# Residual rows of the last but one down group loaded from GpSimd's queue, and the last pair's product placed behind two of that group's additions

## The chip, the cores and the metric

The kernel runs on one core of one Trainium2 chip. The metric is the device time of one execution in microseconds. Engines are named as in the profile: PE is TensorE (matrix products), DVE is VectorE, ACT is ScalarE, POOL is GpSimd, SP is SyncE, which here only issues transfers.

## The reference

One decoder layer over 1040 positions (16 learned ones ahead of 1024) of width 1024: an RMS norm, a mixer (a gated convolution branch and sparse attention, merged and added to the stream), then the convolutional feed-forward part around which this change lies, and a last RMS norm.

```
h = rms_norm(stream, ffn_norm_g[l])
up = causal_depthwise_conv(h @ ffn_up[l], ffn_dw_w[l], ffn_dw_b[l])     # 2 x 2816 columns, width 3
a, b_ = jnp.split(up, 2, axis=-1)
stream = stream + (jax.nn.silu(a) * b_) @ ffn_down[l]
out = rms_norm(stream, final_norm_g)
return out[:, N_META:]
```

## The kernel before

Everything lies channel by partition: a tile is 128 channels by positions. A float32 matrix is split into a high and a low part in TensorE's rounded format, and each product is made in three passes (high x high, high x low, low x high).

**The up part.** The 2816 columns of each half are 22 tiles; tile i of the one half and tile i of the other are a pair. A pair needs seven half-size products (`A11`, `A12`, `A22`, `N2`, `S3`, `S1`, `S4`; the scheme of seven products in place of eight), each of 24 matmuls against the tiles in `B` (`B11`, `B21`, `T4`, `T2`, `T3`, `T1`, `B22`, in this order). `up_pair` adds them up on VectorE into `ua` and `ub`; the last of these additions takes `S4`. `up_rows` makes the rows that the down part reads: three taps of the convolution for each half (the first on ScalarE, L1139, two on VectorE, L1141) into `us` and `ut`, the Silu on `us` (ScalarE, L1142), the product of the halves (VectorE, L1143), a cast of it to the high part `uh` (ScalarE, L1145) and the rest, `ul` (VectorE, L1146).

**The down part.** Two pairs make a group (`GT` = 2), so there are 11 groups. For each group, `down` makes eight products (m = 0 to 7, one for each 128 output channels), each of 12 matmuls of 512 columns, three passes by two pairs by two halves of the positions. Groups 0 to 8 are copied out of PSUM and added in HBM to the residual stream `d_x2` by an accumulating transfer from POOL's queue (L1171). Before group 9, the last but one, `d_x2` is loaded into eight tiles `x2` (named x_0 to x_7 in the profile; L1193), and the products of group 9 (of pairs 18 and 19) are added to them on VectorE (L1167). Group 10, of pairs 20 and 21, comes last and is not made by `down`: it goes in three chunks of positions (384, 384, 256 columns), each followed by its norm and its output, so that a matmul of 384 columns marks its beginning.

**What sets the order.** The instructions of each engine stand in one queue. Which order they get is decided when the program is built, by a planner that follows the data, the priority (the order of the code; `urgent()` raises it by 600 places) and its own estimate of times. Weights pass through `raw` tiles (`d` for the down weights, loaded on SP's queue, L1033) and are split into a ring of five blocks, high part on ScalarE (L1065), low part on VectorE (L1066). PSUM has eight banks, and `slot()` hands out four slots of two banks each in turn, to up and down products alike: the product m + 4 can only begin when the addition of m has read its slot. The tiles `x2` come from a pool of 31 (`ft`) and take the places of the tiles in `B` that are no longer read.

Of the kernel before, what the change touches and what calls it, by code (L numbers as in the profile page):

```python
# [16 lines left out]
ALU = mybir.AluOpType  # L17
# [6 lines left out]
SEQ = 1024  # L24
# [16 lines left out]
GT = 2  # L41
# [39 lines left out]
def body(ctx: ExitStack, tc: tile.TileContext, xT, vecs, w_idx, w_v, w_conv, w_k, w_q, w_gate,  # L81
         w_pw, w_o, w_merge, w_up, w_down, tab128, tab64, topk_rows, mask0, mask_tiny, out):
    nc = tc.nc
    dve, act, pool, pe = nc.vector, nc.scalar, nc.gpsimd, nc.tensor

    def f(t):
        return t.bitcast(F32)

    def urgent():
        return tc.high_priority(offset=600)  # L90
# [8 lines left out]
    def ft(name, dtype=F32):  # L99
        return base.tile([P, FW], dtype, tag="F", bufs=NF, name=name)  # L100

    def tmp(name, dtype=F32):
        return base.tile([P, FW], dtype, tag="T", bufs=4, name=name)
# [10 lines left out]
    def wload(i):  # L114
        src, nk = wlist[i]
        raw = base.tile([P, KT * P], F32, tag="wr", bufs=2, name=f"wr{i}")
        nc.sync.dma_start(raw[:, :nk * P], src)
        wh = base.tile([P, KT * P], F32R, tag="wh", bufs=3, name=f"wh{i}")
        wl = base.tile([P, KT * P], F32R, tag="wl", bufs=2, name=f"wl{i}")
        with urgent():  # L120
            act.copy(wh[:, :nk * P], raw[:, :nk * P])  # L121
            if i < 2 or i >= ix_mg[0][0]:
                placed[0] = dve.tensor_tensor(wl[:, :nk * P], raw[:, :nk * P], f(wh)[:, :nk * P], op=ALU.subtract)
            else:
                act.activation(wl[:, :nk * P], raw[:, :nk * P], AF.Copy, scale=-1.0)
                pool.dma_start(wl[:, :nk * P], src, accum_op=ALU.add)
        wdone[i] = (wh, wl)
# [36 lines left out]
    NPAIR = DFF // P  # L164
# [11 lines left out]
    def c3(ap, w):  # L176
        return ap.rearrange("p (c n) -> p c n", n=w)
# [16 lines left out]
    def psm():  # L194
        turn["mm"] ^= 1
        return PS[:, 3 * turn["mm"]:3 * turn["mm"] + 3, :]

    def bank(key, banks):
        i = turn.get(key, 0)
        turn[key] = i + 1  # L200
        return PS[:, banks[i % len(banks)], :]
# [22 lines left out]
    def vcol(i):  # L224
        return vec[:, i:i + 1]
# [33 lines left out]
    for c in range(NCH):  # L259
# [19 lines left out]
        for k in range(KT):  # L279
            x = xs[k][:, cs]  # L280
# [50 lines left out]
    def rope(ps, ct, st, half, name, c0=0, w=CW, nch=NCH, adder=None):  # L331

        n = w * nch
        sw = tmp(name + "s")
        t = tmp(name + "t")
        with urgent():
            for b in range(0, P, 2 * half):
                act.copy(c3(sw[b:b + half, :n], w), ps[b + half:b + 2 * half, :nch, :w])
                act.copy(c3(sw[b + half:b + 2 * half, :n], w), ps[b:b + half, :nch, :w])
            dve.tensor_tensor(c3(t[:, :n], w), ps[:, :nch, :w], c3(ct[:, c0:c0 + n], w), op=ALU.mult)  # L340
            pool.tensor_tensor(sw[:, :n], sw[:, :n], st[:, c0:c0 + n], op=ALU.mult)
            if adder is None:
                pool.dma_start(t[:, :n], sw[:, :n], accum_op=ALU.add)
            else:
                adder.tensor_tensor(t[:, :n], t[:, :n], sw[:, :n], op=ALU.add)
        return t
# [175 lines left out]
    def table128():  # L522
        if not rt:
            rt[:] = [rope_table("c128", tab128[0]), rope_table("s128", tab128[1])]
        return rt
# [93 lines left out]
    for kind, i, w in units:  # L619
        if kind == "conv":  # L620
            ps = PS[:, 0:3, :] if i == 1 else psm()
# [11 lines left out]
            if i == 0:  # L633
                ps = psa
            else:
                ps = PS[:, 0:3, :] if i == 1 else psm()
                mm(ps, wget(w[1]), hh, hl, KT, LCOLS)
            g = ft(f"g{i}")
# [20 lines left out]
        else:  # L659
            ps = PS[:, 0:3, :] if kind == "g" and i < FILL0 else psm()  # L660
# [6 lines left out]
            elif kind == "k":  # L667
                mm(ps, wget(w), hh, hl, KT, LCOLS)
                t = rope(ps, *table128(), 64, f"kr{i}")
                act.copy(km[:, i * M0:(i + 1) * M0], t[:, :M0])  # L670
                nc.sync.dma_start(d_k[i], t[:, :LC])
            else:
                mm(ps, wget(w), hh, hl, KT, LQCOLS)
                t = rope(ps, *table128(), 64, f"qr{i}", c0=Q0, w=QW)
# [84 lines left out]
    for m in range(KT):  # L759
        tha = load_gate(m)  # L760
        ps = psm()
# [112 lines left out]
    for n in range(len(steps) + 2):  # L874
        if n < len(steps):
            h, p = steps[n]
# [12 lines left out]
    for h in range(NH):  # L889
        a, b = ft(f"oh{h}", F32R), ft(f"ol{h}", F32R)  # L890
# [7 lines left out]
    def ft2(name, dtype=F32):  # L898
        return f2.tile([P, 2 * HB], dtype, tag="F2", bufs=7, name=name)

    def slot():

        turn["sl"] = i = (turn.get("sl", -1) + 1) % 4
        return PS[:, 2 * i:2 * i + 2, :]
# [9 lines left out]
    for m in range(KT):  # L914
        thb, za = load_gate(KT + m), tmp(f"zar{m}")
        nc.sync.dma_start(za[:, :LQ], d_za[m])
        ps = psm()
# [3 lines left out]
        a, b = (ft2 if m == 7 else ft)(f"zh{m}", F32R), (ft2 if m == 7 else ft)(f"zl{m}", F32R)  # L921
# [6 lines left out]
    d_x2 = [dram.tile([P, SEQ], F32, name=f"dx2_{m}") for m in range(KT)]  # L928
# [143 lines left out]
    def block(i, n):  # L1072

        j = count["used"]
        assert bseq[j] == (i, n)
        while count["made"] < min(j + RB, len(bseq)):
            make_block()
        count["used"] += 1
        return ring[j % RB]
# [28 lines left out]
    def up_pair(i):  # L1108

        ua = tmp(f"ua{i}")  # L1110
        if i in early:
            act.copy(ua[:, :2 * HB], early.pop(i)[:, :2 * HB])
        else:
            up_first(i, ua)
        ub = tmp(f"ub{i}")
        U, U2 = ua[:, h1], ub[:, h1]

        def add(dst, a, ps, op=ALU.add):
            with urgent():
                dve.tensor_tensor(dst, a, ps, op=op)  # L1120

        p4 = prod(i, "A22", "T4")
        add(U, U, prod(i, "N2", "T2"), op=ALU.subtract)
        add(U2, U, prod(i, "S3", "T3"))
        add(ub[:, h0], U2, p4)
        p5 = prod(i, "S1", "T1")
        add(U2, U2, p5)
        add(U, U, p5)
        add(U, U, prod(i, "S4", "B22"))
        return ua, ub  # L1130

    def up_rows(i):

        ua, ub = up_pair(i)
        s_, t = ft2(f"us{i}")[:, :SEQ], ft2(f"ut{i}")[:, :SEQ]
        for j, u, d in ((2 * i, ua, s_), (2 * i + 1, ub, t)):
            wc = V_FW + 3 * j
            u, d = u[:, :2 * HB].rearrange("p (c n) -> p c n", n=HB), c3(d, HS)
            act.activation(d, u[:, :, 0:HS], AF.Identity, scale=vcol(wc), bias=vcol(V_FB + j))  # L1139
            for w in (1, 2):  # L1140
                dve.scalar_tensor_tensor(d, u[:, :, w:w + HS], vcol(wc + w), d, op0=ALU.mult, op1=ALU.add)  # L1141
        act.activation(s_, s_, AF.Silu)  # L1142
        dve.tensor_tensor(s_, s_, t, op=ALU.mult)  # L1143
        hi, lo = ft2(f"uh{i}", F32R), ft(f"ul{i}", F32R)
        act.copy(hi[:, :SEQ], s_)  # L1145
        dve.tensor_tensor(lo[:, :SEQ], s_, f(hi)[:, :SEQ], op=ALU.subtract)  # L1146
        return hi, lo

    def down_mm(ps, t, e, rows, c0, w):

        for pi, (o, x) in enumerate(((0, 0), (0, 1), (WB, 0))):
            for k in range(GT):
                for c in range(ps.shape[1]):
                    wo = o + (e * GT + k) * P
                    pe.matmul(ps[:, c, :w], lhsT=t[:, wo:wo + P], rhs=rows[k][x][:, c0 + c * w:c0 + (c + 1) * w],  # L1155
                              start=(pi == 0 and k == 0), stop=(pi == 2 and k == GT - 1))

    def down(g, rows, x2=None):

        for m in range(KT):  # L1160
            ps = slot()
            if m % 2 == 0:
                w = block(g * GT, m // 2)
            down_mm(ps, w, m % 2, rows, 0, HS)
            if x2:
                x = c3(x2[m][:, :SEQ], HS)
                dve.tensor_tensor(x, ps, x, op=ALU.add)  # L1167
            else:
                t = tmp(f"dn{g}_{m}")
                act.copy(c3(t[:, :SEQ], HS), ps)  # L1170
                pool.dma_start(d_x2[m], t[:, :SEQ], accum_op=ALU.add)  # L1171
# [9 lines left out]
    rows_second()  # L1181
    xs2.clear()
    rows = []
    for i in range(NPAIR):
        rows.append(up_rows(i))
        if i % GT == 0 and 0 < i < NPAIR - GT:
            down(i // GT - 1, rows[:GT])
            del rows[:GT]
    B.clear()

    x2 = [ft(f"x2_{m}") for m in range(KT)]
    for m in range(KT):
        nc.sync.dma_start(x2[m][:, :SEQ], d_x2[m])  # L1193
    down(NPAIR // GT - 2, rows[:GT], x2)
    del rows[:GT]


    wd = [block(NPAIR - GT, q) for q in range(4)]
    for c, (c0, nb) in enumerate(DCOLS):
# [4 lines left out]
        for m in range(KT):  # L1204
            ps = bank("dn", (0, 1, 2, 3))
# [105 lines left out]
```

## Time and the profile before

| | us |
|---|---|
| median of 3 runs | 1860.74 (1859.44 to 1862.48) |
| the profiled execution, its own time | 1865.77 |
| its span, from the first instruction to the last | 1863.7 |

The profile is of one execution. Its times are counted from the first instruction; what lies outside the span belongs to the start and the end of the launch. An instruction's length includes its way through the engine, so neighbours on one engine overlap a little: what an instruction costs in a row of equal ones is the distance of two starts. Only idle time of an engine that others wait for costs anything.

### The profile page before, as it was taken

What the parts mean: (1) busy time and instruction counts of PE and PEld (TensorE: products, weight loads), DVE (VectorE), ACT (ScalarE), POOL (GpSimd) and SP (SyncE); (2) the same over time, 40 slices, a digit from 0 to 9 for tenths busy, and PEclk for the clock granted to TensorE, in tenths of its full rate; (3) what the DMA queues carried; (4) which work ended last, traced back from release to release, by engine and by line L of the source; (5) the groups of instructions that cost most, each with busy time, mean ns of one, the idle gap of its engine ahead of it and who ended that gap; (6) DMA issues with size and microseconds to landing.
All of it is one profiled execution on the core that took longest, in us unless ns stands there. A gap on an engine that the chain in (4) does not pass through costs nothing. (4 is left out here: it accounts for less than half of the span.)

```text
span 1863.7 us, 29939 instructions
## 1 busy us (share of the span) xinstructions
PE 1790.6 (96%) x11956; PEld 1719.0 (92%) x11956; DVE 1231.9 (66%) x1949; ACT 1049.3 (56%) x1728; POOL 300.4 (16%) x310
## 2 busy tenths in 40 slices
PE   8989999999999999999999999899999999999987
PEld 7978899999999899899899999888999999999977
DVE  3598588997953472487843467845756575567677
ACT  3565587888999733488832246445434453444334
POOL 0243221111113122121100002011101100110002
PEclk7899999999999999999999999999999999999998
DMA  4434277776656488512246544365446634563432
GB/s 167 91 81 101 59 159 178 177 169 155 147 136 143 129 203 238 137 47 68 70 135 194 176 136 115 107 125 135 103 115 123 147 83 120 116 149 87 105 136 91
DMA packets 83899, 240.10 MB, mean 129 GB/s; under 512 B 8312, under 2 KB 28080, under 8 KB 83760
## 3 DMA queue, kind: packets, MB, share of 16 engines
q0 software_dynamic: 26208, 92.35, 27.9%
q1 hardware_dynamic: 57552, 145.84, 23.5%
q8 instruction: 93, 1.52, 0.3%
q14 instruction: 46, 0.38, 0.1%
HBM read 149.93 MB, written 65.09 MB: 115 GB/s over the span
## 5 line engine op out<-in xcount | busy, mean ns | idle before, releaser
L173 PE MATMUL PS<-hh,wh 128*128 128x342 f32 (+2 forms) x1096 | 196.0, 333 | 15.8 <-DVE qx0t L340 4.8
L1087 PE MATMUL PS<-B,ring 128*128 128x258 f32 (+1 forms) x1584 | 199.4, 286 | 5.5 <-DVE ub L1120 5.5
L1087 PEld LDWEIGHTS PS<-B,ring 128*128 128x128 f32 x1584 | 196.8, 193 | 8.2 <-DVE ub L1120 6.6
L173 PEld LDWEIGHTS PS<-hh,wh 128*128 128x128 f32 x1096 | 183.4, 195 | 20.2 <-DVE qx0t L340 5.2
L1155 PE MATMUL PS<-uh,ring 128*128 128x512 f32 (+2 forms) x736 | 188.6, 389 | 10.4 <-DVE x L1167 6.0
L459 ACT ACTIVATE junk<-sc,wn 128x1040 bf16<-128x1040 f32 (+6 forms) x217 | 182.3, 840 | 26.5 <-DVE wn L483 17.5
L173 PE MATMUL PS<-hh,wl 128*128 128x342 f32 (+2 forms) x1096 | 192.9, 328 | 0.8 <-DMA wl<-w_conv 0.8
L173 PE MATMUL PS<-hl,wh 128*128 128x342 f32 (+2 forms) x1096 | 191.1, 325 | 0.0
L1087 PE MATMUL PS<-h,ring 128*128 128x258 f32 (+1 forms) x1408 | 187.4, 282 | 3.7 <-ACT ring L1065 1.6
L173 PEld LDWEIGHTS PS<-hh,wl 128*128 128x128 f32 x1096 | 181.1, 192 | 2.7 <-DMA wl<-w_conv 1.1
L173 PEld LDWEIGHTS PS<-hl,wh 128*128 128x128 f32 x1096 | 179.4, 190 | 1.6
L1087 PEld LDWEIGHTS PS<-h,ring 128*128 128x128 f32 x1408 | 176.3, 189 | 4.4 <-ACT ring L1065 1.8
L1155 PEld LDWEIGHTS PS<-uh,ring 128*128 128x128 f32 x736 | 136.2, 190 | 39.7 <-issue 6.4
L121 ACT CAST wh<-wr 128x1024 fp32r<-128x1024 f32 x79 | 82.6, 1046 | 141.6 <-PE PS L173 69.5
L554 DVE SCALAR_TENSOR_TENSOR cb<-g,dwh,cb 128x1026 f32<-128x1026 f32 x105 | 138.0, 1316 | 34.8 <-DMA cb<-ct 34.7
L554 DVE SCALAR_TENSOR_TENSOR co<-g,dwh,co 128x1026 f32<-128x1026 f32 x113 | 152.2, 1350 | 1.4 <-ACT co L544 0.6
L1171 POOL DMA_DIRECT2D dx<-dn x72 | 62.4, 871 | 503.4 <-ACT dn L1170 498.0
L1065 ACT CAST ring<-ra 128x512 fp32r<-128x512 f32 x88 | 53.8, 620 | 126.3 <-PE PS L1087 64.6
L1066 DVE TENSOR_TENSOR ring<-ra,ring 128x512 fp32r<-128x512 f32 x88 | 60.0, 687 | 83.4 <-PE PS L1155 42.5
L1155 PE MATMUL PS<-ul,ring 128*128 128x512 f32 (+2 forms) x368 | 103.4, 390 | 0.0
L1087 PE MATMUL PS<-l,ring 128*128 128x258 f32 x704 | 100.1, 284 | 2.3 <-DMA l<-t 2.3
L1065 ACT CAST ring<-rb 128x512 fp32r<-128x512 f32 x66 | 41.0, 621 | 105.3 <-PE PS L1087 38.2
(438 smaller groups left out, 3552.8 us busy)
## 6 DMA issues: line engine op xcount, KB each, us to landing
dx<-dn POOLq DMA_DIRECT2D x72, 512.0 KB, 7.9
ra<-w_up SPq DMA_DIRECT2D x28, 512.0 KB, 3.8
rb<-w_up SPq DMA_DIRECT2D x22, 512.0 KB, 3.7
d<-w_down SPq DMA_DIRECT2D x22, 512.0 KB, 3.6
dth<-gt SPq DMA_DIRECT2D x16, 513.0 KB, 8.0
gate<-dth SPq DMA_DIRECT2D x16, 513.0 KB, 4.2
wr<-w_conv SPq DMA_DIRECT2D x16, 512.0 KB, 4.2
wr<-w_gate SPq DMA_DIRECT2D x16, 512.0 KB, 4.1
```

What stands on the lines that cost most here:

```text
L121: act.copy(wh[:, :nk * P], raw[:, :nk * P])
L173: pe.matmul(ps[:, ci, :n], lhsT=ww[:, sl], rhs=rr[k][:, c0:c0 + n], start=(k == 0 and pi == 0), stop=(k == nk - 1 and pi == 2))
L459: act.activation(junk[:, :n], sc[j][:, PAD:PAD + n], AF.Sign, bias=bits.bitcast(F32)[:, slot[j]:slot[j] + 1], accum_out=cnt[:, slot[j]:slo ...
L554: dve.scalar_tensor_tensor(a, g[:, w:w + LQ], wt[w], a, op0=ALU.mult, op1=ALU.add)
L1065: hi = act.copy(t[:, w0], raw)
L1066: dve.tensor_tensor(t[:, w1], raw, f(t)[:, w0], op=ALU.subtract)
L1087: pe.matmul(ps[:, b, p0:p0 + nn], lhsT=t[:, o + k * P:o + (k + 1) * P], rhs=B[rows][k][e][:, r0:r0 + nn], start=(pi == 0 and k == 0), stop ...
L1155: pe.matmul(ps[:, c, :w], lhsT=t[:, wo:wo + P], rhs=rows[k][x][:, c0 + c * w:c0 + (c + 1) * w], start=(pi == 0 and k == 0), stop=(pi == 2 ...
L1171: pool.dma_start(d_x2[m], t[:, :SEQ], accum_op=ALU.add)
```

## The change

Three edits, all around down group 9 and pair 21, the last. The loads of `x2` go from SP's queue to POOL's. The additions of group 9 are marked urgent. And `up_rows` becomes a generator: for the last pair it stops twice, ahead of the product of the two halves and ahead of `ul`, and `down` resumes it behind m=1 and m=2; by an ordering edge without a wait (`behind`) the product of the halves stands behind the addition of m=1, and `ul` behind that of m=2.

```diff
+    def behind(a, b):
+        tc.add_manual_dep(a.ins, b.ins.name,
+                          mybir.DependencyInfo(mybir.DependencyClass.NoSync, mybir.DependencyReason.DATA), reason="order")
...
-    def up_rows(i):
+    def up_rows(i, adds=None):
...
         act.activation(s_, s_, AF.Silu)
-        dve.tensor_tensor(s_, s_, t, op=ALU.mult)
+        if adds is not None:
+            yield
+        p = dve.tensor_tensor(s_, s_, t, op=ALU.mult)
         hi, lo = ft2(f"uh{i}", F32R), ft(f"ul{i}", F32R)
         act.copy(hi[:, :SEQ], s_)
-        dve.tensor_tensor(lo[:, :SEQ], s_, f(hi)[:, :SEQ], op=ALU.subtract)
-        return hi, lo
+        if adds is not None:
+            behind(p, adds[1])
+            yield
+        p = dve.tensor_tensor(lo[:, :SEQ], s_, f(hi)[:, :SEQ], op=ALU.subtract)
+        if adds is not None:
+            behind(p, adds[2])
+        rows.append((hi, lo))
...
-    def down(g, rows, x2=None):
+    def down(g, rows, x2=None, adds=None, stages=None):
...
             if x2:
                 x = c3(x2[m][:, :SEQ], HS)
-                dve.tensor_tensor(x, ps, x, op=ALU.add)
+                with urgent():
+                    adds.append(dve.tensor_tensor(x, ps, x, op=ALU.add))
+                if m in (1, 2):
+                    next(stages, None)
...
-    for i in range(NPAIR):
-        rows.append(up_rows(i))
+    for i in range(NPAIR - 1):
+        list(up_rows(i))
...
+    adds = []
+    last_pair = up_rows(NPAIR - 1, adds)
+    next(last_pair)
     B.clear()
...
     for m in range(KT):
-        nc.sync.dma_start(x2[m][:, :SEQ], d_x2[m])
-    down(NPAIR // GT - 2, rows[:GT], x2)
+        pool.dma_start(x2[m][:, :SEQ], d_x2[m])
+    down(NPAIR // GT - 2, rows[:GT], x2, adds, last_pair)
```

What the built programs show of the order follows; in front of the tile names stands the line, behind them the shape. The names are those of the code with a running number: `ua_16399`, `ub_16454`, `us_16595`, `ut_16596` and `ul` belong to pair 21, `x_0` to `x_7` are the tiles `x2`, `ring_` the weight blocks, `d_` the loaded down weights.

**First place.** VectorE's queue, before, from the last two half additions of pair 21 (the second of them takes the product `S4`) on:

```order
L1120 TENSOR_TENSOR ua_16399<-ua_16399,PS 128x514 x2
L1066 TENSOR_TENSOR ring_9554<-d_0_16625,ring_9554 128x512
L1066 TENSOR_TENSOR ring_9550<-d_0_16625,ring_9550 128x512
L1141 SCALAR_TENSOR_TENSOR us_16595<-ua_16399,vec,us_16595 128x1024
L1141 SCALAR_TENSOR_TENSOR ut_16596<-ub_16454,vec,ut_16596 128x1024
L1141 SCALAR_TENSOR_TENSOR us_16595<-ua_16399,vec,us_16595 128x1024
L1141 SCALAR_TENSOR_TENSOR ut_16596<-ub_16454,vec,ut_16596 128x1024
L1066 TENSOR_TENSOR ring_9551<-d_2_16683,ring_9551 128x512
L1143 TENSOR_TENSOR us_16595<-us_16595,ut_16596 128x1024
L1146 TENSOR_TENSOR ul_16606<-us_16595,uh_16605 128x1024
L1167 TENSOR_TENSOR x_0_16609<-PS,x_0_16609 128x1024
L1167 TENSOR_TENSOR x_1_16610<-PS,x_1_16610 128x1024
```

VectorE's queue after the change, from the first of these two half additions on:

```order
L1125 TENSOR_TENSOR ua_16399<-ua_16399,PS 128x514
L1181 TENSOR_TENSOR x_0_16604<-PS,x_0_16604 128x1024
L1125 TENSOR_TENSOR ua_16399<-ua_16399,PS 128x514
L1071 TENSOR_TENSOR ring_9554<-d_0_16620,ring_9554 128x512
L1181 TENSOR_TENSOR x_1_16605<-PS,x_1_16605 128x1024
L1071 TENSOR_TENSOR ring_9550<-d_0_16620,ring_9550 128x512
L1147 SCALAR_TENSOR_TENSOR us_16595<-ua_16399,vec,us_16595 128x1024
L1147 SCALAR_TENSOR_TENSOR ut_16596<-ub_16454,vec,ut_16596 128x1024
L1181 TENSOR_TENSOR x_2_16606<-PS,x_2_16606 128x1024
L1147 SCALAR_TENSOR_TENSOR us_16595<-ua_16399,vec,us_16595 128x1024
L1147 SCALAR_TENSOR_TENSOR ut_16596<-ub_16454,vec,ut_16596 128x1024
L1181 TENSOR_TENSOR x_3_16607<-PS,x_3_16607 128x1024
```

All taps, the product of the halves and `ul` stood ahead of the first addition of a residual row; now x_0 stands ahead of the last half addition, x_1 ahead of the taps, and x_2 and x_3 behind one round of taps each.

**Second place.** The rows on VectorE that follow directly, before:

```order
L1167 TENSOR_TENSOR x_2_16611<-PS,x_2_16611 128x1024
L1167 TENSOR_TENSOR x_3_16612<-PS,x_3_16612 128x1024
L1167 TENSOR_TENSOR x_4_16613<-PS,x_4_16613 128x1024
L1066 TENSOR_TENSOR ring_9552<-d_2_16683,ring_9552 128x512
L1167 TENSOR_TENSOR x_5_16614<-PS,x_5_16614 128x1024
L1167 TENSOR_TENSOR x_6_16615<-PS,x_6_16615 128x1024
L1167 TENSOR_TENSOR x_7_16616<-PS,x_7_16616 128x1024
```

And after:

```order
L1071 TENSOR_TENSOR ring_9551<-d_2_16683,ring_9551 128x512
L1181 TENSOR_TENSOR x_4_16608<-PS,x_4_16608 128x1024
L1151 TENSOR_TENSOR us_16595<-us_16595,ut_16596 128x1024
L1181 TENSOR_TENSOR x_5_16609<-PS,x_5_16609 128x1024
L1071 TENSOR_TENSOR ring_9552<-d_2_16683,ring_9552 128x512
L1181 TENSOR_TENSOR x_6_16610<-PS,x_6_16610 128x1024
L1157 TENSOR_TENSOR ul_16652<-us_16595,uh_16651 128x1024
L1181 TENSOR_TENSOR x_7_16611<-PS,x_7_16611 128x1024
L1226 TENSOR_TENSOR x_0_16604<-PS,x_0_16604 128x384
```

The product of the halves (L1151) stands behind x_4 now, `ul` (L1157) behind x_6, and both splits of the last down weights between the additions.

**Third place.** SP's queue, before: the last two loads of down weights and the first three of the residual rows.

```order
L1033 DMA d_0_16625<-w_down 128x4x256
L1033 DMA d_2_16683<-w_down 128x4x256
L1193 DMA x_0_16609<-dx_0_9533 128x1024
L1193 DMA x_1_16610<-dx_1_9534 128x1024
L1193 DMA x_2_16611<-dx_2_9535 128x1024
```

POOL's queue after the change, from the last two accumulating writes of group 8 to its first instruction of the output:

```order
L1187 DMA dx_6_9539<-dn_6_15953 128x1024
L1187 DMA dx_7_9540<-dn_7_15968 128x1024
L1212 DMA x_0_16604<-dx_0_9533 128x1024
L1212 DMA x_1_16605<-dx_1_9534 128x1024
L1212 DMA x_2_16606<-dx_2_9535 128x1024
L1212 DMA x_3_16607<-dx_3_9536 128x1024
L1212 DMA x_4_16608<-dx_4_9537 128x1024
L1212 DMA x_5_16609<-dx_5_9538 128x1024
L1212 DMA x_6_16610<-dx_6_9539 128x1024
L1212 DMA x_7_16611<-dx_7_9540 128x1024
L1249 TENSOR_TENSOR out_0_16839<-x_0_16604,orb_16837 128x384
```

The eight loads have left SP's queue, where two loads of down weights stood ahead of them, and stand on POOL's directly behind the writes of group 8. On TensorE one thing has moved: eight of the twelve matmuls of m=4 stand ahead of those of m=3, and in the first chunk of group 10 the low part of pair 20 stands ahead of that of pair 21. All other rows of TensorE and ScalarE stand as before, but for `uh` of pair 21, which stands behind one weight cast more.

## Rows read from the trace of the kernel before

**Rows 1.** The page of the profile: the span, and the busy time of each engine (us, share of the span, instructions).

```profile
span 1863.7 us, 29939 instructions
...
PE 1790.6 (96%) x11956; PEld 1719.0 (92%) x11956; DVE 1231.9 (66%) x1949; ACT 1049.3 (56%) x1728; POOL 300.4 (16%) x310
```

**Rows 2.** The chain of work that ended last, from 1780 us to the end, in order of time. Columns: start us, length us, engine, tile written, line, number of instructions.

```profile
1795.81 6.30 PE PS L1155 x27
...
1803.24 1.23 DVE us L1143
...
1804.49 1.05 ACT uh L1145
...
1806.71 1.23 DVE x L1167
...
1808.08 25.48 PE PS L1155 x120
```

**Rows 3.** Who waited for whom between 1780 us and the end. Columns: waiting engine and line, releaser, us in total, times, longest us.

```profile
PE PS L1155 <- DVE x L1167: 6.0, 1, 6.0
```

**Rows 4.** The timeline of TensorE around the hole (start us, length us, engine, line, operation, tile written and read, shape, count; in brackets the idle time before and what ended it), and then windows of TensorE (stretch, length, busy us and instructions, granted clock as a share of 2.4 GHz, share of the DMA engines' time, GB/s).

```profile
1787.89 1.09 PE L1155 MATMUL PS<-uh,ring 128*128 128x512 f32 x4
...
1795.65 1.79 PE L1155 MATMUL PS<-uh,ring 128*128 128x512 f32 x7
...
1801.00 1.10 PE L1155 MATMUL PS<-uh,ring 128*128 128x512 f32 x4
...
1808.08 2.05 PE L1155 MATMUL PS<-uh,ring 128*128 128x512 f32 x4 [5.97 <-DVE x L1167]
...
1809.92 1.70 PE L1155 MATMUL PS<-ul,ring 128*128 128x512 f32 x4
...
1811.46 2.02 PE L1155 MATMUL PS<-uh,ring 128*128 128x512 f32 x8
...
1819.84 1.43 PE L1155 MATMUL PS<-uh,ring 128*128 128x512 f32 x6
...
1821.11 0.51 PE L1155 MATMUL PS<-ul,ring 128*128 128x384 f32 x2
```

```profile
1800.00:1802.00 2.00, 2.00 (x9) 1.00 1.02 416
...
1806.00:1808.00 2.00, 0.00 (x0) 0.50 0.00 0
...
1808.00:1810.00 2.00, 1.93 (x5) 0.50 0.00 0
...
1810.00:1812.00 2.00, 2.00 (x8) 0.69 0.00 0
```

**Rows 5.** The timeline of VectorE, columns as for TensorE.

```profile
1776.57 0.69 DVE L1105 TENSOR_TENSOR ua<-ua,PS 128x514 f32<-128x514 f32 x1 [0.87 <-PE PS L1087]
...
1789.64 0.68 DVE L1120 TENSOR_TENSOR ua<-ua,PS 128x514 f32<-128x514 f32 x1
...
1795.85 0.69 DVE L1120 TENSOR_TENSOR ua<-ua,PS 128x514 f32<-128x514 f32 x1 [5.52 <-PE PS L1087]
...
1796.45 1.29 DVE L1066 TENSOR_TENSOR ring<-d,ring 128x512 fp32r<-128x512 f32 x2
...
1797.85 1.28 DVE L1141 SCALAR_TENSOR_TENSOR us<-ua,vec,us 128x1024 f32<-128x1024 f32 x1
...
1802.64 0.69 DVE L1066 TENSOR_TENSOR ring<-d,ring 128x512 fp32r<-128x512 f32 x1
...
1805.57 1.23 DVE L1146 TENSOR_TENSOR ul<-us,uh 128x1024 fp32r<-128x1024 f32 x1 [1.11 <-ACT uh L1145]
...
1806.71 4.61 DVE L1167 TENSOR_TENSOR x<-PS,x 128x1024 f32<-128x1024 f32 x4
...
1820.96 1.23 DVE L1167 TENSOR_TENSOR x<-PS,x 128x1024 f32<-128x1024 f32 x1 [1.57 <-PE PS L1155]
```

**Rows 6.** The timeline of ScalarE, columns as for TensorE.

```profile
1770.82 0.59 ACT L1102 COPY ua<-PS 128x514 f32<-128x514 f32 x1 [0.29 <-PE PS L1087]
...
1778.52 0.63 ACT L1065 CAST ring<-d 128x512 fp32r<-128x512 f32 x1 [0.50 <-ACT ring L1065]
...
1797.72 1.24 ACT L1139 ACTIVATE ut<-ub,vec 128x1024 f32<-128x1024 f32 x1
...
1801.77 1.05 ACT L1142 ACTIVATE us<-us 128x1024 f32<-128x1024 f32 x1
```

**Rows 7.** SP's queue: its timeline around the loads of the residual rows, what it waited for between 1780 us and the end (columns as in rows 3), and of line 1193 (the loads of `x2`) the time from issue to landing.

```profile
1771.61 17.91 SPq L1033 DMA_DIRECT2D d<-w_down  x4
...
1789.61 4.54 SPq L1193 DMA_DIRECT2D x<-dx  x8
```

```profile
SPq L1033 <- DVE ring L1066: 16.2, 3, 8.2
```

```profile
DMA to landing us min/median/max: 7.6/8.9/10.3
```

**Rows 8.** POOL (GpSimd): of line 1171 (the accumulating writes of earlier down groups) the issues, with least, median and longest ns, and their time from issue to landing; and the first instruction of its timeline after the last of these writes.

```profile
L1171 POOL DMA_DIRECT2D dx<-dn x72: 865/865/1209, 1219.9 to 1731.8; - x72
...
DMA to landing us min/median/max: 4.9/7.9/11.4
```

```profile
1842.37 6.47 POOL L1230 TENSOR_TENSOR out<-x,orb 128x384 f32<-128x384 f32 x6 [109.69 <-DVE x L1207]
```

## The prediction

> **What bounds the kernel now.** The page comes first: the span is 1863.7 us, with TensorE busy 96% of it [rows 1]. It is followed by the chain that ended last, in order of time, for the last 84 us. There the chain is TensorE almost without a break, product after product, with one hole: it leaves TensorE at 1802.11 (1795.81 + 6.30), runs over VectorE and ScalarE through the last pair's rows (`us`, `uh`, `ul`) to one addition of a residual row (`x`, L1167), and is back on TensorE at 1808.08 [rows 2]. The list of waits gives the hole a name: TensorE waited once, 6.0 us, for DVE L1167 [rows 3]. The reader should see why. PSUM has four slots, products m=0 to 3 of down group 9 had filled them by 1801.93, and m=4 needs the slot that the addition of m=0 empties. That product was complete at about 1790.7, but its addition ran only at 1806.71, because it stood on VectorE behind everything that makes the last pair's rows [rows 5]. The timeline of TensorE gives the size of the hole, and the windows show a second cost behind it: the granted clock falls to 0.50 (1.2 GHz) in the idle time and stays there for the first products after it [rows 4].
>
> **What the hole costs.** From 1795.65 to 1801.00 TensorE began 23 products of 512 columns, so one takes 0.2326 us. The last four began at 1801.00, the next could have begun at 1801.93, and it began at 1808.08: 6.15 us. Eight products took from 1808.08 to 1811.46, 3.38 us, against 8 x 0.2326 = 1.86 at the full clock: 1.52 us more. Together **7.67 us**, and from 1808.08 the chain is TensorE again (120 products in one piece), so that an earlier start is an earlier end.
>
> **The additions, moved up.** Part by part, first VectorE, on which the forecast rests. In the order of the change the addition of m=0 stands directly behind the half addition of 1789.64, that of m=1 behind the next two instructions, and so on. I set the new order against TensorE's, with starts spaced as the trace has them: 0.60 for a half addition or a ring split, 1.20 for a tap (four from 1797.85 to 1802.64), 1.14 for a row of 1024 (1805.57 to 1806.71) [rows 5].
> TensorE without a hole: m=1 complete at 1796.35, m=2 at 1799.14, eight products of m=4 to 1801.00, m=3 to 1803.79, the rest of m=4 to 1804.72, m=5 1807.51, m=6 1810.30, m=7 1813.09.
> VectorE: x_0 at 1790.9 in time that was idle (5.52 us before 1795.85). Then the last half addition at 1795.85 as before, ring 1796.45, x_1 1797.05, ring 1798.19, two taps to 1801.18, x_2, two taps to 1804.71, x_3, ring 1805.85, x_4 1806.45, the product of the halves 1807.59, x_5 1808.73, ring 1809.87, x_6 1810.5 (its product is complete at 1810.3, and an addition starts some 0.2 behind), `ul` 1811.64, x_7 1813.3 (m=7), done 1814.5.
> Every slot is free before it is wanted: m=5 begins at 1804.72 and x_1 is done at 1798.3; m=6 at 1807.51, x_2 at 1802.4; m=7 at 1810.30, x_3 at 1806.0. The work of 18.2 us that VectorE has from 1795.85 on just fits: the last group's first product begins at 1813.09, needs `uh` of the last pair at once and `ul` six products later. These have 384 columns and take 0.17 us (two between 1820.77 and 1821.11) [rows 4], so `ul` is due at 1814.1, and is done at 1812.9. The slot of x_7 is due twelve products on, at 1815.2, and free at 1814.5. The cover is thus 0.7 to 1.3 us, and each microsecond of lateness beyond it is one lost.
> On ScalarE the taps' first halves end at 1798.96; the Silu (1.05 us) starts behind the second tap of `us`, 1803.6, and is done at 1804.7, before the product of the halves; in the new order one weight cast stands ahead of `uh`, whose weights are read by 1806.6, ahead of the 1808.8 at which `uh` can start [rows 6]. `uh` takes 1.05 [rows 2] and ends at 1809.9. That costs nothing.
>
> **The loads, on another queue.** Before, SP issues them at 1789.61 to 1794.15 behind the fourth load of down weights, since SP waits 16.2 us in three pieces for VectorE's ring splits; they land 7.6 to 10.3 us later, so x_0 not before 1797.2 [rows 7]. With the additions moved up that would be too late. In the built program a load waits for the last product that reads the B11 or B21 tile whose place it takes: these end with the last pair's products A11 and A12, at 1770.8 (ScalarE's copy) and 1776.6 (VectorE's addition) [rows 5, 6]. POOL stands idle from 1732.7 to 1842.37, so nothing is queued in front of the loads or behind them there [rows 8]. An issue on POOL takes 0.87 us: x_0 to x_3 go out from 1770 to 1774, x_4 to x_7 from 1775.9 to 1779.4.
> How long a plain load from POOL's queue takes to land no row shows. The bounds are 4.9 and 11.4 us, of POOL's accumulating writes [rows 8], with SP's 7.6 to 10.3 between; I take 9. x_0 is then there at 1780 (1782 at the upper bound), x_7 at 1788 (1791), against 1790.9 and 1813. The landing costs nothing at either end.
> What the loads meet is a load of down weights issued at 1771.61, whose cast begins at 1778.52. Its split stands on VectorE at about 1781.4, so the cast may start some 2 us later at no cost. At the 416 GB/s that the burst of loads reaches [rows 4], 2.5 MB move in 6 us, to about 1778: zero, at worst 1 us on VectorE, which has 5.5 us idle at 1790.3.
> The Trainium skill ("SBUF — State Buffer", section "SBUF: two separate sides") speaks against the queue: GpSimd cannot write a DMA's descriptors while VectorE runs an instruction in a two-port mode. The row has 865 ns as the least and the median of 72 issues and 1209 as the longest [rows 8], with VectorE busy 66% of the span [rows 1]: no issue was held for long. By the rule an issue may wait out one VectorE instruction, at most 1.28 us, and x_0 would land at 1784 at worst; the sum is the same by either.
>
> **The sum.** -7.67 + 0. In the profiled execution (1865.77, span 1863.7) that is 1858.1 and 1856.0; the profile's run lies 5.0 above the median of the runs, 1860.74. The hole is of work and not of launch, so I take it off the median: **1853.1 us**.
>
> **Rivals.**
> 1. *VectorE becomes the bound.* From 1795.7 on VectorE has 18.2 us of work against 17.4 of TensorE's, so a wait of ScalarE or longer spacings, of 1 to 4 us in total beyond the cover, open a smaller hole in front of the last group. The gain shrinks to 4 to 6.7: 1854.0 to 1856.7. For it: a cover of 0.7. Against it: all spacings are from the same instructions in the same place. 0.13.
> 2. *The queue changes nothing.* The loads land as late as before, x_0 between 1797.2 and 1799.9. VectorE's row of work then starts at 1798.4 to 1801.1 in place of 1795.85, 2.5 to 5.2 late, of which about 1 is covered; the gain is 3.5 to 6.2: 1854.5 to 1857.2. For it: the transfers themselves are the same. Against it: what held them was SP's order (16.2 us of waits) and not the transfer [rows 7]. 0.05. This is what the Trainium skill would have, taken by the letter ("DMA: Bandwidth & Descriptors", section "Issuing engines are not separate DMA queues"): it says that another issuing engine saves only the issue time. No row here shows two queues with the same loads.
> 3. *Something else sets the end.* The tail from 1842 on could start at a time of its own. The chain names none (it goes back to TensorE), so 0.04: 1860.7.
> 4. *Slower.* The addition of x_0 stands on VectorE ahead of the last pair's last half addition. If x_0 lands later than about 1797, each microsecond holds the whole row of 18.2 us, and so TensorE; the gain is gone at 1804.7, 35 us after the issue, and at 1808.4 the kernel is slower by 0.2%, 1864.5. The longest landing from POOL's queue is 11.4. 0.03.
>
> **How the numbers follow.** The forecast has 0.75. Runs of before spread over 3.0 us, so a difference of 0.2% (3.7 us) is about what a measurement of this kernel can tell from no change. The forecast with that spread is 1851.5 to 1854.7. Rivals 1 and 2 reach to 1857, so the range 1850.5 to 1857.0 leaves out about 1 in 10. Faster by over 0.2% means below 1857.0: the forecast, and rivals 1 and 2 but for their ends, 0.89; within 0.2% rival 3 and those ends, 0.07; slower 0.04.
>
> **What the profile after would show.** The row "PE <- DVE x" of 6.0 us is gone from the waits, and the granted clock is 1.00 from 1800 to 1814. x_0 is added at 1790.9, ahead of the half addition of 1795.85, and x_7 at 1813.3. The loads are issued on POOL from 1770 to 1780 and land within 12 us. The first product of 384 columns begins at about 1813, and from there to the end it is the same 43 us as from 1820.77. The forecast is wrong if TensorE waits for `ul` or `x` around 1813, if the half addition starts later than 1795.85, or if a cast of down weights between 1778 and 1788 waits for its load.

## The result and the profile after

| | before | after |
|---|---|---|
| median of 5 runs each, us | 1862.41 (1859.44 to 1864.59) | 1849.34 (1847.82 to 1853.76) |
| ratio after to before | | 0.9939, 95% interval 0.9924 to 0.9953 |
| span of the profiled execution | 1863.7 | 1847.6 |

The kernel became faster, by more than forecast: 1849.34 lies 3.8 us below the 1853.1 of the forecast and 1.2 below the lower end of its range. Twelve more runs of the same program, taken later (below), gave 1852.89 and a ratio of 0.9954.

The page of the changed kernel: the span, and of the line on busy time the engines.

```profile
span 1847.6 us, 29934 instructions
...
PE 1788.0 (97%) x11956; PEld 1717.5 (93%) x11956; DVE 1229.1 (67%) x1949; ACT 1050.1 (57%) x1728; POOL 304.7 (16%) x318
```

TensorE's work is the same 11956 products as in [rows 1]. Its timeline where the hole of [rows 4] was, and windows of it (stretch, length, busy us and instructions, granted clock, DMA share, GB/s):

```profile
1801.97 2.03 PE L1168 MATMUL PS<-uh,ring 128*128 128x512 f32 x8
1803.84 1.09 PE L1168 MATMUL PS<-ul,ring 128*128 128x512 f32 x4
1804.77 1.46 PE L1168 MATMUL PS<-uh,ring 128*128 128x512 f32 x6
1806.06 0.34 PE L1168 MATMUL PS<-ul,ring 128*128 128x384 f32 x1
```

```profile
1800.00:1802.00 2.00, 2.00 (x11) 1.00 0.00 0
...
1804.00:1806.00 2.00, 2.00 (x11) 1.00 0.00 0
1806.00:1808.00 2.00, 2.00 (x14) 1.00 0.00 0
```

No row has a wait, and the clock stays at 1.00 (2.4 GHz) into the last group. Four of the six products from 1804.77 are the last of group 9, at 0.233 each, so the first product of 384 columns begins at 1805.70; in the kernel before it began at 1820.77 [rows 4]. VectorE, in the same stretch:

```profile
1769.15 0.69 DVE L1110 TENSOR_TENSOR ua<-ua,PS 128x514 f32<-128x514 f32 x1 [0.87 <-PE PS L1092]
...
1780.71 0.69 DVE L1071 TENSOR_TENSOR ring<-d,ring 128x512 fp32r<-128x512 f32 x1 [1.94 <-ACT ring L1070]
...
1784.85 1.22 DVE L1181 TENSOR_TENSOR x<-PS,x 128x1024 f32<-128x1024 f32 x1
1788.43 0.69 DVE L1125 TENSOR_TENSOR ua<-ua,PS 128x514 f32<-128x514 f32 x1 [2.35 <-PE PS L1092]
...
1804.25 1.22 DVE L1157 TENSOR_TENSOR ul<-us,uh 128x1024 fp32r<-128x1024 f32 x1
1805.91 1.23 DVE L1181 TENSOR_TENSOR x<-PS,x 128x1024 f32<-128x1024 f32 x1 [0.44 <-PE PS L1168]
```

The addition of x_0 (1784.85) now stands ahead of the last half addition (1788.43), and x_7 (1805.91) waits for its product, not for VectorE. Two executions are best laid over each other by a landmark that the change does not touch: VectorE's addition of the product A12 of pair 21, 1776.57 before [rows 5] and 1769.15 here. The last half addition stands 19.28 us behind it in both (1795.85 and 1788.43), though TensorE then goes on at once in one and stops in the other.

**Where the 16.1 us between the two spans come from.** 7.42 lie ahead of the landmark (1776.57 - 1769.15), where both programs hold the same instructions in the same order, but for the loads on GpSimd's queue that have begun by then; 8.69 lie behind it (87.10 and 78.41 to the end). Of the part behind, 7.65 are gone at the first product of 384 columns (1820.77 - 1805.70 = 15.07, less 7.42), and 1.0 goes in the tail (where it goes stands under "The size" below).

The part ahead shows how far it is from the change. Windows of TensorE from 40 to 60 us, before, after, and in a further execution of the program before (e1, below):

```profile
40.00:60.00 20.00, 20.00 (x99) 0.58 0.00 1
```

```profile
40.00:60.00 20.00, 20.00 (x117) 0.74 0.01 1
```

```profile
40.00:60.00 20.00, 20.00 (x126) 0.83 0.00 1
```

TensorE was busy all 20 us in each, and was granted 0.58, 0.74 and 0.83 of its clock. The same group of 15 products starts behind it at 62.24, 58.15 and 56.33: 4 us between before and after, and 6 between two executions of one program.

The new sides of the change. GpSimd's timeline, then of line 1212 (the loads of `x2`) the issues and the time from issue to landing, and what ScalarE waited for between the landmark and the end:

```profile
1762.94 2.14 POOL L1212 DMA_DIRECT2D x<-dx  x4 [37.67 <-PE PS L1092]
1768.69 2.08 POOL L1212 DMA_DIRECT2D x<-dx  x4 [3.61 <-PE PS L1092]
```

```profile
L1212 POOL DMA_DIRECT2D x<-dx x8: 527/528/563, 1762.9 to 1770.2; - x8
...
DMA to landing us min/median/max: 4.0/6.3/8.6
```

```profile
ACT ring L1070 <- DMA d<-w_down: 6.1, 2, 4.5
```

The loads go out behind the products A11 and A12 and land within 8.6 us. The last row is a wait that the kernel before did not have: one cast of down weights stood 4.5 us for its load (another 1.6), and this is what the 1.94 us of idle time at 1780.71 on VectorE come from. VectorE was idle for another 2.35 in front of 1788.43, so nothing behind it moved.

### The profile page after: what moved, and what is told of

Its sections match the earlier page's. It is cut to its first block, busy times and chain, and to the rows that moved or that the text cites. A ratio compares the mean times of both kernels' runs of the same rounds, so it can differ in the third digit from the quotient of the medians.

```text
span 1847.6 us, 29934 instructions
## 1 busy us (share of the span) xinstructions
PE 1788.0 (97%) x11956; PEld 1717.5 (93%) x11956; DVE 1229.1 (67%) x1949; ACT 1050.1 (57%) x1728; POOL 304.7 (16%) x318
## 3 DMA queue, kind: packets, MB, share of 16 engines
q8 instruction: 93, 1.52, 0.3%
```

## The experiments

Theory A: the gain is VectorE's order alone; the loads only have to be there in time. Its rivals: the queue is what counts (B), the urgency or the edges are (C), the difference is in part one between two executions and not of the change (D). In the table the landmark is the one above, and what stands behind it is compared, since what is ahead of it belongs to no edit: the landmark lies at 1771.9 us on the mean of the four traces with the old order and at 1772.3 on that of the seven with the new. The kernels e6 to e9 have one run each and are read from their traces alone.

| kernel | runs | median us | before beside it | ratio (95%) | landmark | landmark to end |
|---|---|---|---|---|---|---|
| before (first profile) | 5 | 1862.41 | | | 1776.57 | 87.10 |
| after (first profile) | 5 | 1849.34 | 1862.41 | 0.9939 (0.9924 to 0.9953) | 1769.15 | 78.41 |
| e1_same | 12 | 1859.00 | 1861.83 | 0.9991 (0.9976 to 1.0006) | 1767.90 | 87.26 |
| e2_whole | 12 | 1852.89 | 1861.83 | 0.9954 (0.9939 to 0.9969) | 1772.25 | 78.38 |
| e3_queue_only | 12 | 1860.53 | 1861.83 | 0.9995 (0.9982 to 1.0007) | 1772.86 | 86.88 |
| e4_order_only | 8 | 1854.31 | 1861.83 | 0.9958 (0.9942 to 0.9974) | 1774.86 | 78.79 |
| e5_split_only | 9 | 1853.44 | 1861.15 | 0.9963 (0.9947 to 0.9979) | 1772.54 | 78.77 |
| e6_urgent_only | 1 | 1860.04 | 1861.15 | | 1770.40 | 87.53 |
| e7_ul_twice | 1 | 1858.03 | 1861.15 | | 1777.22 | 79.04 |
| e8_ul_four_times | 1 | 1858.51 | 1861.15 | | 1773.00 | 83.74 |
| e9_late_loads | 1 | 1847.37 | 1860.66 | | 1767.23 | 78.36 |

### The same program again (e1), and the change again (e2)

No edit: the kernel before as it stands, and the changed kernel as it stands.

> The kernel before, unchanged. The result shows 13.1 us between the medians, the forecast had 7.7. Theory A: the surplus is scatter of the runs in stretches that the change does not touch. Then two sets of runs of one program can differ by some us: the ratio here lies within 0.9980 to 1.0020, and in the profile the landmark (VectorE's addition L1105 of pair 21, at 1776.57 in the trace of before and at 1769.15 in that of after) moves by several us, while the time from it to the end stays at 87.1. Theory B: the surplus belongs to the change. Then the landmark stays at 1776 to 1777 here and the ratio is 1.0000 within 0.0005.

> The change once more, in new runs beside before. Theory A (a gain of 7.7 at the hole and up to 1 in the tail, the rest scatter): ratio 0.9950 to 0.9965, landmark anywhere, from it to the end 78.4 to 79.5 us. Theory B (the change is worth 11 to 13 us): ratio 0.9925 to 0.9945 again, and the landmark some 7 us ahead of that of e1_same.

e1 measured 0.9991 and has its landmark 8.67 us earlier than the first profile of the very same program. That is more than the 7.42 of the first pair, so this part needs no effect of the change (D). e2 measured 0.9954: by this ratio 8.6 us of the 1861.83 beside it, against 13.1 in the first five runs; behind the landmark it agrees with the first profile of after to 0.03 us. TensorE around the hole in e1:

```profile
1792.33 1.10 PE L1155 MATMUL PS<-uh,ring 128*128 128x512 f32 x4
1799.41 2.05 PE L1155 MATMUL PS<-uh,ring 128*128 128x512 f32 x4 [5.98 <-DVE x L1167]
1801.25 1.91 PE L1155 MATMUL PS<-ul,ring 128*128 128x512 f32 x4
1802.96 2.70 PE L1155 MATMUL PS<-uh,ring 128*128 128x512 f32 x8
1805.49 1.09 PE L1155 MATMUL PS<-ul,ring 128*128 128x512 f32 x4
```

and a window of it (columns as in the result):

```profile
1804.00:1806.00 2.00, 2.00 (x10) 0.89 0.00 0
```

The stop is the one of [rows 4]: from 1793.26 (1792.33 + 4 x 0.2326) to 1799.41, 6.15. But the stretch of low clock behind it is longer. Sixteen products take 6.08 us (1805.49 - 1799.41) against 3.72 at full speed: 2.36, where the first profile had 1.52. e3 and e6, which have the hole too, had 1.64 and 2.63 by the same count. What differs is when the clock comes back. A share of 0.89 for this window puts the step from 0.50 to 1.00 at about 1804.4, 5.0 us behind TensorE's new start; in the first profile it was 3.2 us (0.69 for 1810 to 1812 [rows 4]), in e3 3.4 and in e6 5.6, and the products lost nearly half of that each time. The hole is thus worth 7.7 to 8.8, by how long the lower level still lasts when TensorE goes on, and I had priced it from the shortest of four.

### The queue alone (e3) and the order alone (e4)

e3 is the kernel before with

```diff
-        nc.sync.dma_start(x2[m][:, :SEQ], d_x2[m])
+        pool.dma_start(x2[m][:, :SEQ], d_x2[m])
```

and e4 the changed kernel with it turned back:

```diff
-        pool.dma_start(x2[m][:, :SEQ], d_x2[m])
+        nc.sync.dma_start(x2[m][:, :SEQ], d_x2[m])
```

> Only the loads of the residual rows go to GpSimd's queue; the additions keep their old place behind the last pair's rows. The theory of the prediction: the loads land by 1790 instead of 1797 to 1803, but the addition of x_0 still stands at 1806.7, so that the wait of TensorE for DVE x of 6.0 us and the low clock behind it remain: ratio 0.9985 to 1.0015, from the landmark to the end 87. Rival (the late loads were what held the additions): the wait shrinks by some us.

> The new order of the additions, with the loads left on SP's queue. The prediction's step: with SP's queue x_0 lands at 1797.2 to 1799.9, behind the 1795.85 of the last half addition, and 1.3 to 4 us of the gain are lost: from the landmark to the end 80 to 83.5. Rival: in this build the loads stand on SP's queue ahead of the last load of down weights, behind one that was issued at 1784.5, so they are issued from 1785 on, x_0 lands at 1792.5 to 1795.2, and the gain is the whole one: 78.4 to 79.5 from the landmark to the end, the same ratio as e2_whole.

The waits of e3 between 1775 us and the end:

```profile
PE PS L1155 <- DVE x L1167: 6.0, 1, 6.0
...
ACT ring L1065 <- DMA d<-w_down: 4.3, 2, 3.6
```

The queue alone leaves the hole as it was, with the residual rows in place long before (issued from 1766.89 on, 7.5 us at most to land), and brings the new wait for down weights. e4 has the whole gain but for 0.4 us behind the landmark: the rival that stands in its expectation came, not the step of the prediction. Its SP queue, the time from issue to landing of its loads of `x2`, and three rows of its VectorE:

```profile
1769.91 13.22 SPq L1038 DMA_DIRECT2D d<-w_down  x3
1783.23 3.93 SPq L1212 DMA_DIRECT2D x<-dx  x8
1787.78 0.38 SPq L1038 DMA_DIRECT2D d<-w_down  x1
```

```profile
DMA to landing us min/median/max: 7.4/8.6/9.8
```

```profile
1774.86 0.69 DVE L1110 TENSOR_TENSOR ua<-ua,PS 128x514 f32<-128x514 f32 x1 [0.87 <-PE PS L1092]
...
1789.18 1.23 DVE L1181 TENSOR_TENSOR x<-PS,x 128x1024 f32<-128x1024 f32 x1 [0.57 <-PE PS L1168]
1794.14 0.69 DVE L1125 TENSOR_TENSOR ua<-ua,PS 128x514 f32<-128x514 f32 x1 [3.74 <-PE PS L1092]
```

Two things made SP's queue early enough. With the additions ahead, the planner put the loads in front of the last load of down weights instead of behind it: 8.37 us behind the landmark, where it was 13.04 before [rows 5, 7]. And x_0 was there sooner than I had read from the row of landings. The addition that reads x_0 began 5.95 us after the first issue, having waited for TensorE alone; in e5 it was 5.96. The row is not of all eight loads: in e4 the trace holds the landing of two, the fifth (7.4) and the eighth (9.8), and the 7.6 and 10.3 of before [rows 7] are those of the fourth and the seventh. Such a row is no lower bound for the first load of a burst, which is how I had used it. There is no wait for a load of down weights in e4 at all; the wait in after belongs to the loads' new place.

The Trainium skill ("DMA: Bandwidth & Descriptors", section "Issuing engines are not separate DMA queues") has another issuing engine save only the issue time. e3 (ratio 0.9995) and e4 against e2 (0.4 us) agree with it in that the queue is worth next to nothing. The 0.4 us are there in every trace, but not at the loads: from TensorE's broadcast of the last chunk's norm to the end it takes 8.2 us in the five traces with the loads on SP's queue (8.18 to 8.20) and 7.8 in the six with them on GpSimd's (7.79 to 7.83). Why the end of the program is shorter there is not shown. B is left with these 0.4 us.

### Which part of the order (e5, e6)

e5 is the kernel before with the generator and its two stops only: loads on SP, no `urgent()`, no `behind`.

```diff
-                with urgent():
-                    adds.append(dve.tensor_tensor(x, ps, x, op=ALU.add))
+                adds.append(dve.tensor_tensor(x, ps, x, op=ALU.add))
...
-            behind(p, adds[1])
...
-            behind(p, adds[2])
```

(against the changed kernel, with the loads on SP as in e4). e6 is the kernel before with the urgency alone:

```diff
-                dve.tensor_tensor(x, ps, x, op=ALU.add)
+                with urgent():
+                    dve.tensor_tensor(x, ps, x, op=ALU.add)
```

> The stages of the last pair alone: the generator stops twice as in the change, but the loads stay on SP's queue, the additions are not urgent and there are no ordering edges. In the built order x_0 stands ahead of the last half addition, x_1 ahead of the taps, x_2 and x_3 between and behind them, nearly as in the change. Theory (the place of the additions is the whole gain, and it comes from the order of the code): 78.4 to 79.5 us from the landmark (VectorE's addition of the last pair's A12) to the end, no wait of TensorE for x, ratio 0.993 to 0.997. Rival (each part carries a share): 80 to 85.

> The additions of group 9 marked urgent, and nothing else of the change. In the built order they still stand behind the last pair's ul, as before. Theory: nothing is gained, 86.5 to 87.5 us from the landmark to the end, and TensorE waits 6.0 us for DVE x. Rival (urgency moves them up on the chip): under 85.

e5 keeps the gain (78.77, ratio 0.9963). e6 has none; TensorE's wait in it:

```profile
PE PS L1155 <- DVE x L1168: 6.0, 1, 6.0
```

Urgency leaves the first addition 30.15 us behind the landmark, where it was 30.14. What moves it is the order of the code: the product of the halves and `ul` are written behind m=1 and m=2. On VectorE e5 differs from e4 in three places only, where a weight split and an addition have changed places, and the two end within 0.02 us of each other (78.77 and 78.79). C falls, for urgency and edges both.

### How near the new order is to its own limit (e7, e8, e9)

e7 and e8 make `ul` of the last pair once more and three times more (the same subtraction, 1.14 us each; e8 has 3 where e7 has 1):

```diff
+        for _ in range(1 if adds is not None else 0):
+            p = dve.tensor_tensor(lo[:, :SEQ], s_, f(hi)[:, :SEQ], op=ALU.subtract)
```

> The change, with the subtraction that makes the last pair's ul done twice (1.14 us more on VectorE, the same values). It measures the cover that the prediction gave as 0.7 to 1.3 us: x_7 is then added at 1814.4 (by the clock of the trace of before) and its slot is due at 1815.2 and free at 1815.6, so that TensorE stops for 0.4 us at most: from the landmark to the end 78.4 to 79.0. Rival (there is no cover, VectorE is the bound already): 79.5.

> The change, with the subtraction that makes ul done four times (3.4 us more on VectorE). With a cover of 1 us TensorE stops for 2.2 to 2.7 us in front of the last group, and the granted clock may fall behind it as it did in the hole of before: 80.6 to 82.5 us from the landmark to the end. Rival (more cover than the prediction has): 79 to 80.

The last `ul`, x_7 and the repeats on VectorE, in e7 and then in e8:

```profile
1812.33 1.22 DVE L1157 TENSOR_TENSOR ul<-us,uh 128x1024 fp32r<-128x1024 f32 x1
1813.99 1.23 DVE L1183 TENSOR_TENSOR x<-PS,x 128x1024 f32<-128x1024 f32 x1 [0.44 <-PE PS L1170]
1815.13 1.22 DVE L1159 TENSOR_TENSOR ul<-us,uh 128x1024 fp32r<-128x1024 f32 x1
```

```profile
1809.77 1.23 DVE L1183 TENSOR_TENSOR x<-PS,x 128x1024 f32<-128x1024 f32 x1 [0.44 <-PE PS L1170]
1810.91 3.74 DVE L1159 TENSOR_TENSOR ul<-us,uh 128x1024 fp32r<-128x1024 f32 x3
```

The planner put the repeats behind x_7, which begins 36.77 us behind the landmark in both, as in after (36.76). So neither kernel delays x_7, and neither measures the cover that the expectations speak of; what comes late is the last `ul`. In e7 TensorE waits once for VectorE:

```profile
PE PS L1170 <- DVE x L1183: 0.3, 1, 0.3
```

The planner changed the order of the first products of group 10 too, so that TensorE stood at the slot of x_7 after some six of them instead of twelve. e7 has 79.04 us to the end, just above the 78.4 to 79.0 expected and 0.6 more than after and e2 (78.4), all of it ahead of the first chunk's norm broadcast. In e8, TensorE and its windows:

```profile
1812.04 0.34 PE L1170 MATMUL PS<-ul,ring 128*128 128x384 f32 x1
1814.70 0.51 PE L1170 MATMUL PS<-ul,ring 128*128 128x384 f32 x1 [2.32 <-DVE ul L1159]
1815.01 0.84 PE L1170 MATMUL PS<-uh,ring 128*128 128x384 f32 x2
```

```profile
1812.00:1814.00 2.00, 0.38 (x3) 1.00 0.00 0
1814.00:1816.00 2.00, 1.30 (x5) 0.73 0.00 0
1816.00:1818.00 2.00, 2.00 (x8) 0.50 0.00 0
1818.00:1820.00 2.00, 2.00 (x12) 0.91 0.00 0
```

Stops of 0.27 (for x_7, as in e7) and 2.32 us (for the last `ul`), and yet 5.3 us more to the end. The clock was still 1.00 up to 1814; a share of 0.73 for the next window puts its fall to 0.50 at about 1814.9, 0.2 us behind TensorE's new start, and the products from there on took 0.32 us instead of 0.175. By the norm broadcast of the first chunk, 60.90 us behind the landmark (56.24 in after), 4.66 are lost: 2.6 of standing and 2.1 of slow products; the rest comes later, in the second broadcast (1.65 us against 0.94). The 83.74 to the end are 1.2 above the upper end of what was expected.

e9 makes the loads late. On GpSimd a copy of one column stands in front of each:

```diff
+        pool.tensor_copy(x2[m][:, :1], last_ub[0][:, HB:HB + 1])
         pool.dma_start(x2[m][:, :SEQ], d_x2[m])
```

> The changed kernel, but on GpSimd a copy of one column from ub of the last pair stands ahead of the eight loads of the residual rows, so that they cannot start before the last addition to ub has been made, 15.2 us behind the landmark (VectorE's addition of the last pair's product A12); in the changed kernel they are issued at 6.2 us ahead of the landmark and up to it. All else keeps its place but two neighbours on VectorE. Theory (the additions in their new place are the gain, and the loads only have to be there in time): x_0 is issued about 16 us behind the landmark and lands 4 to 8.6 us later (the issue-to-landing times of the changed kernel), at 20 to 24.6; to be free it would have to be there at 18.1, one addition ahead of the half addition at 19.3. VectorE therefore waits for a load by 1.9 to 6.5 us, about 1 of it covered, and TensorE stops for 1 to 5.5 us in front of the last group: from the landmark to the end 79.3 to 84 us in place of 78.4. Rival (the moment of the loads does not matter, the rows are wanted later than I think): 78.4 to 78.8, and no wait of VectorE for a load.

Rows of e9's VectorE:

```profile
1767.23 0.69 DVE L1110 TENSOR_TENSOR ua<-ua,PS 128x514 f32<-128x514 f32 x1 [0.87 <-PE PS L1092]
...
1786.24 1.22 DVE L1183 TENSOR_TENSOR x<-PS,x 128x1024 f32<-128x1024 f32 x1 [5.25 <-DMA x<-dx]
1787.38 0.68 DVE L1125 TENSOR_TENSOR ua<-ua,PS 128x514 f32<-128x514 f32 x1
...
1804.23 1.22 DVE L1183 TENSOR_TENSOR x<-PS,x 128x1024 f32<-128x1024 f32 x1
```

VectorE did wait for the load of x_0, 5.25 us, and the half addition came 20.15 us behind the landmark in place of 19.28. Those 0.87 us cost nothing: 78.36. The theory's time was missed, and the rival's came (78.4 to 78.8), though not for its reason, since VectorE did wait for a load. The theory missed because I took the issue for 2 us later than it was: in after the last addition to `ub` itself comes late, held by the split whose weights waited for their load, and with the loads later that wait is gone (e9 has no wait for a load of down weights). So a half addition that comes 0.87 us late is covered; x_7 began 0.24 us later than in after. What a later landing than this costs (the fourth rival) was not tried.

## Why the prediction was right, and where not

**The mechanism** was right in each step that carries the sum. The wait of [rows 3] is gone, the granted clock is 1.00 from 1800 to 1808, x_0 stands ahead of the half addition and x_7 where forecast (36.76 behind the landmark, forecast 1813.3 - 1776.57 = 36.7). The gain up to the first product of 384 columns is 7.65, forecast 7.67, and VectorE's row of work just fits, as it was laid out: `ul` done 0.23 us ahead of the first product of group 10, x_7 done at 1807.14 (1805.91 + 1.23) against a slot due at 1807.8, a cover of 0.7 at the tighter end (forecast 0.7 to 1.3).

**The size.** The term that was mis-sized is the 1.52 us of slow products. It is not one number: 1.52, 2.36, 1.64 and 2.63 in four executions with the hole, 2.0 on the mean. A second part lies in the tail, which the prediction had as the same 43 us. TensorE's broadcasts of the norms of the second and the third chunk, before and then after:

```profile
1848.91 1.65 PE L247 MATMUL PS<-ident,on1r 128*128 128x128 f32 x6 [2.12 <-DVE on1r L242]
1855.49 1.22 PE L247 MATMUL PS<-ident,on2r 128*128 128x128 f32 x4 [3.43 <-DVE on2r L242]
```

```profile
1833.88 0.94 PE L252 MATMUL PS<-ident,on1r 128*128 128x128 f32 x6 [2.07 <-DVE on1r L247]
1839.74 1.22 PE L252 MATMUL PS<-ident,on2r 128*128 128x128 f32 x4 [2.98 <-DVE on2r L247]
```

The first row of before is 0.7 us longer. The granted clock had fallen to 0.50 just ahead of it, as in e3 and e8, which have 1.65 too; in the other eight traces the clock fell behind it. Old and new order are on both sides of this, so it is no effect of the order; why the clock fell earlier is not settled. The other 0.4 us are the end of the program, behind the second row, which goes with the queue (above). From the landmark on the change gives 8.9 us (87.30, the mean of before, e1 and e6, less 78.40, the mean of after and e2), not 7.67. The stop of 6.15, 2.2 of slow products, 0.2 of the slow broadcast (0.7 in one of the three) and 0.4 of the queue add up to it within 0.1. With the loads on SP's queue the gain is 8.5 (e4 and e5 have 78.78).

**The number in the result.** 13.07 us of medians is more than that by 4.2, and no part of the change was found for it. By their ratios e2, e4 and e5 give 8.6, 7.8 and 6.9, and one program's landmark moves by 8.7 us from one execution to another. The step of the prediction that failed is the sentence that sets the range: it took the spread of three runs, 3.0 us, for that of the kernel. The 31 runs of before beside e1 to e4 went from 1856.1 to 1869.0, and the first five runs of after have a median 3.5 us below that of the twelve of e2. A range drawn from those would have reached lower. That e2's 1852.89 lies 0.2 us from the forecast is in part luck: the 1860.74 that it started from was 1.1 below the median of the 31, and the gain was taken 1.2 too small, so that the two errors cancel.

**The loads.** "With the additions moved up that would be too late" was wrong, twice over: SP's order is the planner's and moved with the additions, and "not before 1797.2" was read from a row that does not hold the landing of x_0 (e4). The forecast did not hang on it. What the rival "the queue changes nothing" says holds but for 0.4 us; its price does not, since the gain without the queue is 8.5 and not 3.5 to 6.2. The issue on GpSimd took 0.53 us, not 0.87: plain loads are issued faster than the accumulating writes of [rows 8]. The landing, 4.0 to 8.6, lay a little below my bounds. No issue was held by VectorE for long (563 ns the longest), so what the Trainium skill says of a starved GpSimd queue ("SBUF — State Buffer", section "SBUF: two separate sides") did not show here either.

**The contention** came, and it reached one load further than I looked. The load of 1771.61 (here 1764.19) held its cast 1.6 us, so that it began 3.06 us behind the landmark in place of 1.95, at no cost, as forecast. The next, issued at 1772.86, held its cast 4.5 us. That took 1.94 us of VectorE, where the prediction had 1 at worst, and x_0 came 15.70 us behind the landmark in place of the 14.3 forecast (14.32 in e4, which has no such wait). VectorE had another 2.35 us idle behind it. One of the signs that I had named for a wrong forecast was there and cost nothing, because VectorE's idle time in front of the last half addition was the cover that the prediction had named for it.

## What to carry to other kernels

Where TensorE waits for a slot of PSUM, look at what stands ahead of the emptying addition on its engine: here the order of the code alone, one stage of the last pair written behind the next products, gave 8.5 of the 8.9 us, and neither priority nor edges were needed. Price a hole as the stop plus the slow products behind it, and take the second from several executions. Before a row of landings is used as a bound, look whether it holds the load in question. Compare two traces from a landmark that the change cannot touch: without it, 7.4 us of difference from other stretches would have been put down to the edit.

## What the runs showed of the hardware

A stop of TensorE of 2.3 us in e8 cost nearly twice its length by the next norm broadcast, since the granted clock was 0.50 (1.2 GHz) for the products behind it; behind the stop of 6.15 us the slow products cost 1.5 to 2.6 more. Early in the program, from 40 to 60 us, TensorE was busy without a break in three executions and was granted 0.58, 0.74 and 0.83 of its clock, two of them of one program. Eight plain loads of 512 KB from GpSimd's queue were issued at 0.53 us each and landed in 4.0 to 8.6 us; a load of 512 KB on SP's queue issued 2.6 us behind the last of them held its reader until 7.2 us after its issue (1772.86 to 1780.05), where the 18 of 72 loads of that line whose landing the trace holds took 3.5 at the median.
